# A whole encoder block on one core: later steps for the linear heads' functions, other pages for the embedding, another start of the value weights, and two moved hand-overs

## The chip, the core and the metric

The kernel runs as one program on one core of one Trainium2 chip. The metric is the device time of one execution in microseconds (us). In the views of the profile PE is the engine of matrix products, ACT and DVE are the two engines of elementwise work, POOL is a third one that is little used here, and SP issues most of the transfers between HBM and the on-chip memory (SBUF). Everything is fp32.

## The reference

One layer of an encoder over 512 frames of 2048 values:

```python
h = rms_norm(x, norm_mix_w)
q_a, k_a, v_a, q_g, k_g, v_g, r_g, gate_lr = split_cols(h @ w_in, IN_SPLITS)
y_a = chunked_band_attention(...)          # 16 heads of 64, a learned bias by distance
log_a = log_sigmoid(gate_lr @ w_gla_gate_up + b_gla_gate) / 16
o_g = gated_linear_attention(q_g, k_g, v_g, log_a)      # 4 heads, chunks of 64
y_g = rms_norm(o_g, gla_norm_w) * silu(r_g)
x = x + concatenate([y_a, y_g]) @ w_out
h = rms_norm(x, norm_ffn_w)
u = causal_depthwise_conv(h @ w_ffn_up, w_ffn_conv, b_ffn_conv)   # width 3, 11264 channels
u_gate, u_val = split(u, 2)
x = x + (gelu(u_gate) * u_val) @ w_ffn_down
g = sigmoid(rms_norm(x, norm_ple_w) @ w_ple_gate)
x = x + g * (p @ w_ple_proj)               # the embedding
return rms_norm(x, final_norm_w)
```

## The kernel before

**Products.** A product of large matrices is cut into units of 256 output columns (of the weight's 128-column blocks, two of them), and a unit is computed by seven block products instead of eight, with sums and differences of quarters of the weight and of the input. The seven are P1, P2, P6, P5, P7, P3, P4 in this order. Each needs one block of weights (L11, L12, S1 to S4, L22: quarters or their sums) and one operand made from the input (R11, R21, N1, N2, T3, R22, T4). An operand is kept in two halves of four tiles, g = 0 and g = 1. In the programs' names in_T, up_R or dn_N are such operands of the stages in, up and dn; accA, accB and accC are the three accumulators; u is a unit's output page.

**Splits.** To reach fp32 accuracy each block of weights (a page `l` or `s`) and each operand is split into a high part, which ACT copies, and a low part, which DVE makes by a subtraction. Both go into one page `wsplit` of a ring of three (w0 to w2), starting at a float of the page that SHIFT gives: 3 for ordinary units, 29 for value units (kind "v"), 48 for the embedding and for the first projection of the values (wtile). The pages themselves start at multiples of 64 bytes. Each block product is then 24 matmuls of 128x128 by 256 columns: high by high, high by low, low by high for eight tiles.

**Stages.** In order: the first projection (rows with L239 to L241) with the input norm; the low-rank gate; the stage `linear` (units 16, 20, 21, 17, 22, 23, 18, 8, 19, of which 20 to 23 are value units, in which the split weight is the streamed operand of the matmul); `front` (attention units 0 to 7 and units 9 to 11); the embedding (four units, PSUM tiles `pp`, output pages `pp_o`, stored to a scratch `ppd` in HBM); `wo`, the output projection; `up` with 44 units and a convolution (pages `cv`); `dn0`, `dn1`, `dn2`, the three parts of the down projection; `pg`, the gate of the embedding; the last norm. The stages wo, up and pg are chained: the last two column blocks of an operand's half g = 1 are not loaded from scratch but split straight from the tiles of the units just computed ("tails").

**What sets the order.** The main loop runs over steps, one block product each. Everything else is put into an agenda: a list of (k, function) for each step. In a step the functions with k = 0 come first, then the high part of the weight two steps ahead (ACT), then the functions with k from 1 to under 2, then its low part (DVE), then the product (PE), then the functions with larger k, then the collect, in which ACT copies or DVE adds the accumulator into the page u. ACT, DVE and PE keep the order in which the program is written. SP's transfers are ordered by the scheduler of the tile layer from the same program, and a transfer waits on SP for its data and its page.

**What is touched.** `gla_head` gives the functions of a linear head: `load_v`, `logits`, `softplus` (e: Abs, Exp, Ln), `least`, `sums` (a scan into cs), `powers` (eb, en, dd, dec: exponentials of cs), `decays`, each at a step of its unit (`gates_begin`); then the head's products from `normed` to `result`, with the root of its norm (`root`: Ln and Exp; `root_exact`), and at last the store of the head's output (ond). `after_up` gives a unit of up its scaling, the three taps of its convolution, Gelu, the gate and the store. `embedding` copies the sums of `pp` into `pp_o`. `attend` is the attention of a front unit, with its bias page. A table at the end of front places wo's operands (`kept` is the half whose page holds the embedding's input `ps` until then). Rings of pages are named by tags: u0 to u3, c0 to c2, r0 to r8, w0 to w2, x0, x1.

Of the kernel before, what the change touches and what calls it, by code (L numbers as in the profile page):

```python
# [34 lines left out]
SHIFT = {"v": 29, "pp": 48}  # L35
# [8 lines left out]
def encoder_block(ctx: ExitStack, tc: tile.TileContext, A, out):  # L44
# [604 lines left out]
    def after_up(unit):  # L649
        f = unit.u  # L650

        def scale():
            vec.tensor_tensor(unit.o, unit.o, rb2, ALU.mult)
            unit.c = page("c", "cv").rearrange("p (s t) -> p s t", s=2)

        def tap(s, j):
            blk = s * FB + f
            u, c = unit.o[:, s, :], unit.c[:, s, :]
            if j == 2:
                act.activation(c, u, AF.Identity, scale=cw[:, blk, 2:3], bias=cw[:, blk, 3:4])  # L660
            else:
                d = 2 - j
                vec.scalar_tensor_tensor(c[:, d:], u[:, :T - d], cw[:, blk, j:j + 1], c[:, d:], ALU.mult, ALU.add)

        def gate():
            g = unit.c[:, 1, :]
            vec.tensor_tensor(g, unit.c[:, 0, :], g, ALU.mult)

        def join():
            ci, k, second = unit.slot  # L670
            if second:
                store_pair(gd[ci], k, held[0], unit.c[:, 1, :])
            else:
                held[0] = unit.c[:, 1, :]

        return [(0, 1, scale), (0, 2, lambda: [tap(0, 2), tap(1, 2)]), (1, 1, lambda: [tap(0, 1), tap(0, 0)]),
                (1, 2, lambda: act.activation(unit.c[:, 0, :], unit.c[:, 0, :], AF.Gelu_apprx_tanh)),
                (2, 1, lambda: [tap(1, 1), tap(1, 0)]), (3, 1, gate), (4, 1, join)]
# [39 lines left out]
    def embedding(unit):  # L718

        hi, lo = unit.w["PP"]  # L720
        for i in range(4):
            if i % 2 == 0:
                o = page("c", "pp_o").rearrange("p (s t) -> p s t", s=2)
# [14 lines left out]
    def attend(unit):  # L738
# [6 lines left out]
        def load_e():  # L745
            for s in range(2):
                nc.sync.dma_start(bias[0][:, s, :], A["bias"][2 * b + s])
# [136 lines left out]
    def gla_head(unit):  # L884
# [11 lines left out]
        def softplus():  # L896
# [3 lines left out]
            act.activation(e, e, AF.Ln, bias=1.0)  # L900
# [13 lines left out]
        def powers():  # L914
            for n, k in (("eb", 1.0), ("en", -1.0)):
                M[n] = gt(n, n)
                act.activation(M[n], M["cs"], AF.Exp, scale=k / TAU)
            act.activation(M["dd"], M["dd"], AF.Exp, scale=-1.0 / TAU)
# [11 lines left out]
        def gates_begin():  # L930
            i = base[unit]
            for t, k, f in ((0, 0, load_v), (0, 6, logits), (1, 2, softplus), (1, 3, least), (2, 1, sums), (2, 2, powers),
                            (4, 1, decays)):
                agenda[i + t].append((k, f))
# [77 lines left out]
        def root():  # L1012
            M["rg"] = gt("rg", "cs")
            act.activation(M["rg"], M["ms"], AF.Ln, scale=1.0 / 256, bias=epst)
            act.activation(M["rg"], M["rg"], AF.Exp, scale=-0.5)
# [9 lines left out]
        def result():  # L1025
            for vb in range(2):
# [6 lines left out]
                (7, 3, root_exact), (8, 1, result), (10, 0, lambda: nc.sync.dma_start(ond[hd], M["o"]))]  # L1033
# [65 lines left out]
    for a, b in zip(stages[3:], stages[4:]):  # L1099
        i0 = base[a.units[-1]]  # L1100
        for n, p in enumerate(PLAIN):
            op = PRODUCTS[p][1]
            for g in range(2):
# [4 lines left out]
                if g and b.chained and op in ("R21", "T4"):  # L1108
                    at = max(at, 15)
# [13 lines left out]
    for n, p in enumerate(PLAIN):  # L1123
        op = PRODUCTS[p][1]
        for g in range(2):
            kept = (op, g) == ("N1", 1)
            agenda[i0 + (11 if kept else n + 1)].append((0, lambda op=op, g=g: wo.load(op, g)))
            agenda[i0 + (13 if kept else n + 4)].append((3, lambda op=op, g=g: wo.split(op, g, True, (0,) if g else ())))
        at, k = ((9, 1), (9, 1), (10, 1), (14, 1), (13, 3), (14, 3), (15, 3))[n]
# [13 lines left out]
    agenda[i0 + 5].append((1, lambda: embedding_split(raws["p"], xtile("N1", 1, "ps"))))  # L1143
# [181 lines left out]
    def open_attention():  # L1325
        gctx.close()
        att.append(actx.enter_context(tc.tile_pool(name="att", bufs=1, side="right", reuse_waits="tile")))
        bias.append(pg.tile([P, 2, T], F32, tag="r7", name="bias"))

    agenda[base[front.units[0]] + 8].append((1.5, open_attention))  # L1330
# [187 lines left out]
```

## Time and profile before

| | us |
|---|---|
| median of 3 runs | 2262.68 (2260.53 to 2263.29) |
| profiled execution | 2261.3 |
| its span, first to last instruction | 2259.6 |
| PE busy | 2202.8 (97%) |
| DVE busy | 1938.2 (86%) |
| ACT busy | 1345.1 (60%) |
| mean granted clock of PE | 0.992 |

In the rows of a timeline the first number is the start in us from the span's start, the second the duration, then the engine, the line, the operation, and the tiles it writes and reads; x24 is the number of equal instructions in a run; what stands in brackets is the idle time of the engine before it and what ended it. Most instructions have line 64, a helper that records them, so the tiles tell them apart. For matmuls the first tile behind the arrow is the streamed operand, the second the stationary one. A row's duration ends after the last matmul's drain, so the spacing of matmuls is taken from one start to the next.

### The profile page before, as it was taken

Reading aid. Unit: us, or ns where it says so; the run is one execution under the profiler, and the core shown is the slowest. Engines: PE = TensorE matmul, PEld = TensorE weight load, DVE = VectorE, ACT = ScalarE, POOL = GpSimd, SP = SyncE. Lnnn points to the kernel's source line nnn. Section 1 sums busy time; section 2 is a strip of 40 time slices with the busy share of each in tenths; the row PEclk is TensorE's granted clock in tenths of the full one; section 3 lists DMA queues with packets and bytes.
Section 4 is the critical chain, followed back from the end, with each engine's and each line's share of the span. In section 5 each row is a group of like instructions: output and inputs, shape, how many; then the busy total and the mean of one; then the engine's idle time right before and its main releaser. Section 6 shows DMA issues by size and latency. Waiting matters only on the chain.

```text
span 2259.6 us, 46287 instructions
## 1 busy us (share of the span) xinstructions
PE 2202.8 (97%) x18588; PEld 2151.8 (95%) x18588; DVE 1938.2 (86%) x2655; ACT 1345.1 (60%) x2001; POOL 158.3 (7%) x196
## 2 busy tenths in 40 slices
PE   9999999999999999999999999999999999999995
PEld 8899988999989999999999999999999999999995
DVE  8476778999869898999888898889898797999997
ACT  9455556777666565555555555555564554766655
POOL 0000000000000010000000100000000100000000
PEclk9999999999999999999999999999999999999998
DMA  7466755677888987888888888888866967879994
GB/s 245 128 186 177 212 154 155 188 189 194 286 266 268 309 243 202 225 226 224 222 215 223 215 224 216 215 225 214 266 208 232 310 243 252 302 254 329 277 300 158
DMA packets 190760, 518.31 MB, mean 229 GB/s; under 512 B 20272, under 2 KB 66608, under 8 KB 190544
## 3 DMA queue, kind: packets, MB, share of 16 engines
q1 hardware_dynamic: 160272, 415.72, 54.1%
q0 software_dynamic: 25920, 93.33, 23.1%
q10 hardware_dynamic: 4352, 6.29, 0.8%
q8 instruction: 146, 2.39, 0.4%
q14 instruction: 70, 0.57, 0.1%
HBM read 441.86 MB, written 71.30 MB: 227 GB/s over the span
## 4 chain that ended last, share of the span: by engine, by line
PE 79%; DVE 8%; DMA 7%; ACT 3%; issue 2%; SPq 0%; ACTq 0%; DVEq 0%; POOLq 0%
PE accA L64 40%; PE accC L64 21%; PE accB L64 10%; DVE wsplit L64 2%; PE v L239 1%; PE v L240 1%; PE v L241 1%; DVE u L64 1%; DMA dn_R<-g_R 1%; PE py L64 1%; DMA ppd<-pp_o 1%; PE ptr L64 1%; DMA l<-in_w_ple_gate 1%; PE psc L64 1%; DMA pg_T<-h_T 1%
## 5 line engine op out<-in xcount | busy, mean ns | idle before, releaser
L64 ACT ACTIVATE wsplit<-l 128x1024 fp32r<-128x1024 f32 (+1 forms) x476 | 495.3, 1041 | 301.7 <-PE accC L64 129.8
L64 DVE TENSOR_TENSOR wsplit<-l,wsplit 128x1024 fp32r<-128x1024 f32 (+1 forms) x476 | 571.0, 1201 | 110.3 <-ACT wsplit L64 109.4
L64 DVE TENSOR_TENSOR wsplit<-s,wsplit 128x1024 fp32r<-128x1024 f32 (+1 forms) x253 | 303.5, 1201 | 59.6 <-ACT wsplit L64 59.1
L64 ACT ACTIVATE wsplit<-s 128x1024 fp32r<-128x1024 f32 (+1 forms) x253 | 262.5, 1038 | 62.1 <-PE accB L64 33.4
L64 ACT ACTIVATE u<-accA 128x256 f32<-128x256 f32 x302 | 113.8, 377 | 265.6 <-PE accA L64 265.5
L64 PE MATMUL accA<-up_T,wsplit 128*128 128x256 f32 x2112 | 253.2, 276 | 0.0
L64 PEld LDWEIGHTS accA<-up_T,wsplit 128*128 128x128 f32 x2112 | 245.6, 188 | 0.1
L64 DVE SCALAR_TENSOR_TENSOR cv<-u,cw,cv 128x511 f32<-128x511 f32 (+1 forms) x176 | 131.5, 747 | 3.1
L64 PE MATMUL accB<-up_R,wsplit 128*128 128x256 f32 x1056 | 129.3, 279 | 2.6 <-ACT up_R L64 1.4
L64 PE MATMUL accA<-dn_T,wsplit 128*128 128x256 f32 x1056 | 126.8, 277 | 3.8 <-DVE wsplit L64 2.1
L405 POOL DMA_DIRECT2D s<-in_w_up x88 | 76.1, 865 | 765.6 <-DMA s<-in_w_up 460.4
L64 PEld LDWEIGHTS accB<-up_R,wsplit 128*128 128x128 f32 x1056 | 124.9, 190 | 3.4 <-ACT up_R L64 1.6
L64 PEld LDWEIGHTS accA<-dn_T,wsplit 128*128 128x128 f32 x1056 | 122.8, 188 | 4.8 <-DVE wsplit L64 2.7
L64 PE MATMUL accA<-up_R,wsplit 128*128 128x256 f32 x1056 | 126.9, 276 | 0.0
L64 PE MATMUL accC<-up_R,wsplit 128*128 128x256 f32 x1056 | 126.5, 276 | 0.0
L64 PE MATMUL accA<-up_N,wsplit 128*128 128x256 f32 x1056 | 126.5, 276 | 0.0
L64 PE MATMUL accC<-up_N,wsplit 128*128 128x256 f32 x1056 | 126.5, 276 | 0.0
L64 PEld LDWEIGHTS accA<-up_R,wsplit 128*128 128x128 f32 x1056 | 122.9, 188 | 0.5 <-ACT u L64 0.2
L64 PEld LDWEIGHTS accC<-up_N,wsplit 128*128 128x128 f32 x1056 | 122.8, 188 | 0.0
L64 PEld LDWEIGHTS accC<-up_R,wsplit 128*128 128x128 f32 x1056 | 122.8, 188 | 0.0
L64 PEld LDWEIGHTS accA<-up_N,wsplit 128*128 128x128 f32 x1056 | 122.8, 188 | 0.0
L64 PE MATMUL accA<-in_T,wsplit 128*128 128x256 f32 x768 | 97.8, 284 | 9.0 <-ACT u L64 7.5
(337 smaller groups left out, 4244.2 us busy)
## 6 DMA issues: line engine op xcount, KB each, us to landing
l<-in_w_up SPq DMA_DIRECT2D x132, 512.0 KB, 4.5
s<-in_w_up SPq DMA_DIRECT2D x88, 512.0 KB, 5.0
s<-in_w_up POOLq DMA_DIRECT2D x88, 512.0 KB, 6.0
l<-in_w_dn SPq DMA_DIRECT2D x56, 448.0 KB, 5.2
l<-in_w_blk SPq DMA_DIRECT2D x48, 512.0 KB, 4.6
s<-in_w_blk SPq DMA_DIRECT2D x32, 512.0 KB, 4.4
s<-in_w_blk POOLq DMA_DIRECT2D x32, 512.0 KB, 7.6
l<-in_w_out SPq DMA_DIRECT2D x28, 512.0 KB, 5.1
```

The costliest lines, as they stand in the source:

```text
L64: ins = f(*args, **kw)
L239: nc.tensor.matmul(ps[t], x[:, 0, sl], wh, start=kt == 0, stop=False)
L240: nc.tensor.matmul(ps[t], x[:, 0, sl], wl, start=False, stop=False)
L241: nc.tensor.matmul(ps[t], x[:, 1, sl], wh, start=False, stop=kt == KD - 1)
L405: nc.gpsimd.dma_start(t, src("L22" if name == "S1" else "L11"), accum_op=ALU.add)
```

## The change

1. Value units' split weights start at float 32 of their page instead of 29.
2. For the last three units of up, whose work goes into the start of dn0, the scaling, the taps, Gelu, the gate and the store come up to two steps later or are spread.
3. The embedding's second output page of unit 0 is taken from tag u0, and that of unit 1 from u3. The other six rotate through c0 to c2.
4. The bias page of the attention is taken at the first load of a bias, and the pool of the attention opens at step 9 instead of 8.
5. In a linear head, softplus' logarithm is a function of its own, half a step later; the sums go from (2, 1) to (3, 1); the powers from (2, 2) to (4, 1), with dd and dec apart at (4, 3); the decays from (4, 1) to (6, 1). The root's exponential is a function of its own at (8, 1); root_exact, the result and the store come a step later each.
6. The embedding's input lies in the second half of T3 instead of N1, so that N1's half is loaded early and T3's at step 14, with its split after step 16.
7. In up and pg the split of R21's second half comes after step 14 instead of 15.

The diff:

```diff
-SHIFT = {"v": 29, "pp": 48}
+SHIFT = {"v": 32, "pp": 48}
...
+        if unit.pos - len(unit.stage.units) in unit.stage.late:
+            return [(0, 1, scale), (1, 1, lambda: [tap(0, 2), tap(1, 2)]), (2, 1, lambda: [tap(0, 1), tap(0, 0)]),
+                    (3, 1, lambda: act.activation(unit.c[:, 0, :], unit.c[:, 0, :], AF.Gelu_apprx_tanh)),
+                    (3, 3, lambda: [tap(1, 1), tap(1, 0)]), (4, 1, gate), (5, 1, join)]
         return [(0, 1, scale), (0, 2, lambda: [tap(0, 2), tap(1, 2)]), (1, 1, lambda: [tap(0, 1), tap(0, 0)]),
                 (1, 2, lambda: act.activation(unit.c[:, 0, :], unit.c[:, 0, :], AF.Gelu_apprx_tanh)),
                 (2, 1, lambda: [tap(1, 1), tap(1, 0)]), (3, 1, gate), (4, 1, join)]
...
-                o = page("c", "pp_o").rearrange("p (s t) -> p s t", s=2)
+                spare = {(0, 2): (pg, "u0"), (1, 2): (late[0], "u3")}.get((unit.u, i))
+                o = (spare[0].tile([P, 1024], F32, tag=spare[1], name="pp_o") if spare else page("c", "pp_o")).rearrange("p (s t) -> p s t", s=2)
...
         def load_e():
+            if not bias:
+                bias.append(pg.tile([P, 2, T], F32, tag="r7", name="bias"))
...
-            act.activation(e, e, AF.Ln, bias=1.0)
+
+        def logs():
+            act.activation(M["e"], M["e"], AF.Ln, bias=1.0)
...
+
+        def falls():
             act.activation(M["dd"], M["dd"], AF.Exp, scale=-1.0 / TAU)
...
-            for t, k, f in ((0, 0, load_v), (0, 6, logits), (1, 2, softplus), (1, 3, least), (2, 1, sums), (2, 2, powers),
-                            (4, 1, decays)):
+            for t, k, f in ((0, 0, load_v), (0, 6, logits), (1, 2, softplus), (1, 3, least), (2, 2, logs), (3, 1, sums),
+                            (4, 1, powers), (4, 3, falls), (6, 1, decays)):
...
             act.activation(M["rg"], M["ms"], AF.Ln, scale=1.0 / 256, bias=epst)
+
+        def rooted():
             act.activation(M["rg"], M["rg"], AF.Exp, scale=-0.5)
...
-                (7, 3, root_exact), (8, 1, result), (10, 0, lambda: nc.sync.dma_start(ond[hd], M["o"]))]
+                (8, 1, rooted), (8, 3, root_exact), (9, 1, result), (11, 0, lambda: nc.sync.dma_start(ond[hd], M["o"]))]
...
-                    at = max(at, 15)
+                    at = max(at, 14 if op == "R21" else 15)
...
-            kept = (op, g) == ("N1", 1)
-            agenda[i0 + (11 if kept else n + 1)].append((0, lambda op=op, g=g: wo.load(op, g)))
-            agenda[i0 + (13 if kept else n + 4)].append((3, lambda op=op, g=g: wo.split(op, g, True, (0,) if g else ())))
-        at, k = ((9, 1), (9, 1), (10, 1), (14, 1), (13, 3), (14, 3), (15, 3))[n]
+            kept = (op, g) == ("T3", 1)
+            agenda[i0 + (14 if kept else n + 1)].append((0, lambda op=op, g=g: wo.load(op, g)))
+            agenda[i0 + (16 if kept else n + 4)].append((3, lambda op=op, g=g: wo.split(op, g, True, (0,) if g else ())))
+        at, k = ((9, 1), (9, 1), (10, 1), (12, 1), (16, 3), (14, 3), (15, 3))[n]
...
-    agenda[i0 + 5].append((1, lambda: embedding_split(raws["p"], xtile("N1", 1, "ps"))))
+    agenda[i0 + 5].append((1, lambda: embedding_split(raws["p"], xtile("T3", 1, "ps"))))
...
-        bias.append(pg.tile([P, 2, T], F32, tag="r7", name="bias"))
-
-    agenda[base[front.units[0]] + 8].append((1.5, open_attention))
+
+    agenda[base[front.units[0]] + 9].append((1.5, open_attention))
```

Where it moves instructions, at three places.

ACT in unit 19, the last of the stage linear, from the split for P6 on. Before (rg is the root of the head before, e the softplus of this one, eb to dec its powers; u<-u is the gate's Silu, u<-accA the collects of P1 and P6):

```order
L64 ACT_TABLE_LOAD
L64 ACTIVATE rg<-rg 128x512
L64 ACT_TABLE_LOAD
L64 ACTIVATE u<-u 128x1024
L64 ACTIVATE u<-accA 128x256
L64 ACTIVATE wsplit<-s_2885 128x1024
...
L64 ACTIVATE wsplit<-s_2926 128x1024
L64 ACT_TABLE_LOAD
L64 ACTIVATE eb<-cs 128x512
L64 ACTIVATE en<-cs 128x512
L64 ACTIVATE dd<-dd 128x512
L64 ACTIVATE dec<-cs 128x8
L64 ACTIVATE u<-accA 128x256
```

And in the changed kernel:

```order
L64 ACT_TABLE_LOAD
L64 ACTIVATE u<-u 128x1024
L64 ACTIVATE u<-accA 128x256
L64 ACTIVATE wsplit<-s_2885 128x1024
L64 ACT_TABLE_LOAD
L64 ACTIVATE rg<-rg 128x512
...
L64 ACTIVATE e<-e 128x512
L64 ACTIVATE u<-accA 128x256
L64 ACTIVATE wsplit<-l_2719 128x1024
L64 ACTIVATE u<-accC 128x256
...
L64 ACTIVATE eb<-cs 128x512
```

The root's exponential has moved behind the collect of P1, and the powers from ahead of P6's collect to behind P5's.

DVE at the start of up, where the tails of the operands' second halves are split. Before:

```order
L64 TENSOR_TENSOR up_N_9121<-up_N_9121 128x1024
L64 TENSOR_TENSOR l_8982<-l_8982,s_9092 128x1024
L64 SCALAR_TENSOR_TENSOR tp<-tp,u 128x256
L64 TENSOR_TENSOR wsplit<-l_9059,wsplit 128x1024
L64 TENSOR_TENSOR up_R_9021<-up_R_9021 128x512
L64 TENSOR_TENSOR up_R_9021<-u,up_R_9021 128x256 x2
L64 TENSOR_TENSOR up_N_9087<-up_N_9087 128x512
```

In the changed kernel:

```order
L64 TENSOR_TENSOR up_R_9021<-up_R_9021 128x512
L64 TENSOR_TENSOR up_R_9021<-u,up_R_9021 128x256 x2
L64 TENSOR_TENSOR up_N_9121<-up_N_9121 128x1024
L64 TENSOR_TENSOR l_8982<-l_8982,s_9092 128x1024
L64 SCALAR_TENSOR_TENSOR tp<-tp,u 128x256
L64 TENSOR_TENSOR wsplit<-l_9059,wsplit 128x1024
L64 TENSOR_TENSOR up_N_9087<-up_N_9087 128x512
```

R21's split (up_R) has moved ahead of a whole operand half, a sum of weights and a weight's low part; the rows are the same ones.

ACT at the hand-over from up to dn0, around the splits for P7 of the first pair. Before:

```order
L64 ACTIVATE cv<-u,cw 128x512 x2
L64 ACTIVATE dn_T_19450<-dn_T_19450 128x1024
L64 ACTIVATE u<-accA 128x256
L64 ACTIVATE wsplit<-s_19387 128x1024
L64 ACTIVATE cv<-cv 128x512
L64 ACTIVATE dn_T_19548<-dn_T_19548 128x1024
```

In the changed kernel:

```order
L64 ACTIVATE dn_T_19450<-dn_T_19450 128x1024
L64 ACTIVATE u<-accA 128x256
L64 ACTIVATE wsplit<-s_19387 128x1024
L64 ACTIVATE cv<-u,cw 128x512 x2
L64 ACTIVATE dn_T_19548<-dn_T_19548 128x1024
```

The convolution's first taps (cv<-u,cw) stand behind the split of T3 and of the weight instead of ahead of them, and Gelu (cv<-cv) has gone further back.

## The prediction

> **What bounds it now.** I read the page's engine shares first, then the chain that ended last, then PE's timeline for every place where the spacing of matmuls is above the usual.
>
> ```profile
> PE 2202.8 (97%) x18588; PEld 2151.8 (95%) x18588; DVE 1938.2 (86%) x2655; ACT 1345.1 (60%) x2001; POOL 158.3 (7%) x196
> PE 79%; DVE 8%; DMA 7%; ACT 3%; issue 2%; SPq 0%; ACTq 0%; DVEq 0%; POOLq 0%
> ```
>
> PE is the bound of the whole: PE's order and its count of matmuls do not change, so only two things can move the end: matmuls that run closer together, and waits of PE that go away or come new. The change is five such edits, and I price each where it acts.
>
> **Value units (start of the halves 29 to 32 floats).** In a value unit the split weight is the streamed operand, written first in a row's pair; in the others it is the stationary one.
>
> ```profile
> 92.75 0.39 PE L239 MATMUL v<-wv_s,in_R 128*128 128x512 f32 x1
> ...
> 95.24 0.39 PE L241 MATMUL v<-wv_s,in_R 128*128 128x512 f32 x1
> ...
> 109.44 2.88 PE L64 MATMUL accA<-in_N,wsplit 128*128 128x256 f32 x24
> 112.16 2.88 PE L64 MATMUL accC<-in_N,wsplit 128*128 128x256 f32 x24
> ...
> 156.04 5.92 PE L64 MATMUL accA<-wsplit,in_T 128*128 128x256 f32 x48
> 161.80 5.92 PE L64 MATMUL accC<-wsplit,in_R 128*128 128x256 f32 x48
> ```
>
> Ordinary: 112.16 − 109.44 = 2.72 us for 24, 113.3 ns each. Value: 161.80 − 156.04 = 5.76 for 48, 120.0 ns. The excess of 6.7 ns is 1/17 of 113.3, the time of about 15 of 256 columns, or some 60 bytes of a row: as if one 64-byte piece more were read because the row starts inside a piece. The pages start at multiples of 64 bytes; 29 floats are 116 bytes, which is no multiple, 32 are 128, which is. The first projection supports this: there too a split weight is streamed, out of the same pages, but from float 48 (192 bytes), and eleven steps take 95.24 − 92.75 = 2.49 us, 226 ns per 512 columns, 113 per 256. So it is not the streaming of a split weight as such. There are 4 units x 7 products x 24 = 672 such matmuls: 672 x 6.7 ns = **4.5 us**. Bounds: 0 (another cause) and 4.5. I take 4.5.
>
> The Trainium skill, "TensorE: Matmul & The Clock Gate", "Back-to-back issue gap", gives N / 2.4 + 2.5 ns for a warm matmul, 109.2 for 256 columns, with no term for the start address; the rows' 113.3 and 120.0 are both above it. By that rule this edit is worth 0, which is rival A.
>
> **Gates and heads of the linear units.** In each of these units PE's P7 waits for ACT, which is in a run of table loads, logarithms and exponentials ahead of the collect of P6.
>
> ```profile
> 115.83 2.99 PE L64 MATMUL accA<-in_T,wsplit 128*128 128x256 f32 x24 [0.78 <-ACT u L64]
> 182.90 2.88 PE L64 MATMUL accC<-in_N,wsplit 128*128 128x256 f32 x24
> 185.93 3.03 PE L64 MATMUL accA<-in_T,wsplit 128*128 128x256 f32 x24
> ...
> 310.13 5.45 PE L64 MATMUL accA<-in_T,wsplit 128*128 128x256 f32 x24 [5.06 <-ACT u L64]
> 315.41 2.90 PE L64 MATMUL accC<-in_R,wsplit 128*128 128x256 f32 x24
> ```
>
> Unit 16 loses 115.83 − 112.16 − 2.72 = 0.95, unit 17 185.93 − 182.90 − 2.72 = 0.31, and I give unit 18 the same: 1.6 us. The same ACT items spread over later steps can hide behind the products P5 to P4, whose steps have none of them now; their readers, the products with keys and queries, come a unit later. I take 1.6 (bounds 0.5 and 1.6). The last unit, 19, is the large one: the wait of 5.06, and then 24 matmuls in 315.41 − 310.13 = 5.28 instead of 2.72, at half clock. It also carries the root of the head before. ACT's rows there, and one stretch with each engine's busy time (PE, PEld, DVE, ACT):
>
> ```profile
> 297.96 1.06 ACT L64 ACTIVATE u<-u 128x1024 f32<-128x1024 f32 x1
> 298.93 0.36 ACT L64 ACTIVATE u<-accA 128x256 f32<-128x256 f32 x1
> 308.03 0.63 ACT L64 ACTIVATE eb<-cs 128x512 f32<-128x512 f32 x1 [1.08 <-DVE cs L64]
> 309.71 0.36 ACT L64 ACTIVATE u<-accA 128x256 f32<-128x256 f32 x1
> ...
> 297.00:310.00 13.00, 7.63 (x65) 7.23 (x64) 12.65 (x18) 11.83 (x17) 0.86 (x1) 0.95 0.53 158
> ```
>
> Between the two collects (298.93 and 309.71) ACT now has 10.8 us. After the change the powers with their wait for the sums (308.03 to 309.71 and 1.08 ahead, 2.8 us) and a table load come behind P5's collect, and the root's exponential comes between the two collects instead of before the first, with a table load fewer there since Exp follows Exp: P1's collect moves to about 297.0, P6's to about 304.6, and P7 starts near 304.8 and at full clock. But the stretch shows DVE busy for 12.65 of 13.00 us: the same work must still pass DVE. From the gate's multiply to P7's low half it has 11.3 us of rows, so that half is done near 308.4, and P7's last 8 matmuls wait 1.9 us, P3's about 1 more. Front's first matmul falls at about 316.4 instead of 320.87: **4.4 us** (bounds 2.5, if the two new waits cost half clock too, and 5.0).
>
> **Front's second unit.** Head 19's tail falls under it, and a DVE queue that waits for a transfer:
>
> ```profile
> 361.91 3.00 PE L64 MATMUL accA<-in_T,wsplit 128*128 128x256 f32 x24 [1.63 <-ACT u L64]
> 370.44 3.12 PE L64 MATMUL accA<-in_T,wsplit 128*128 128x256 f32 x24 [1.19 <-DVE u L64]
> ...
> 368.65 0.17 DVE L64 MEMSET bias<- 64x128 f32 x1 [1.56 <-PE accC L64]
> ...
> 356.77 0.33 SPq L1033 DMA_DIRECT2D ond<-og  x1
> 360.93 0.86 SPq L747 DMA_DIRECT2D bias<-in_bias x2
> ```
>
> The 1.63 goes. But the head's result and its store (ond) move a step later: counted from front's start as before, I place the store at about 359.4, and the bias load stands behind it on SP, with a weight load and va's. On DVE the mask (368.65) waits for that load, and behind the mask P4's low half, P7's collect and P3's low half are queued; PE's P4 waits for them. With the landing at about 369 P4 starts near 371.1 where it was 370.44: **−0.7** (bounds −2.0, and +2.9 if the load lands as now).
>
> **Embedding and wo.** ACT copies the embedding's sums into pages of a ring whose stores have not landed yet, and PE waits for ACT:
>
> ```profile
> 618.20 5.74 PE L64 MATMUL pp<-ps,wsplit 128*128 128x512 f32 x24 [1.47 <-ACT pp_o L64]
> 625.86 7.32 PE L64 MATMUL pp<-ps,wsplit 128*128 128x512 f32 x24 [1.92 <-ACT pp_o L64]
> 634.81 3.02 PE L64 MATMUL pp<-ps,wsplit 128*128 128x512 f32 x12 [1.63 <-ACT pp_o L64]
> 638.36 3.02 PE L64 MATMUL pp<-ps,wsplit 128*128 128x512 f32 x12 [0.54 <-ACT pp_o L64]
> 641.22 5.62 PE L64 MATMUL accA<-wo_R,wsplit 128*128 128x256 f32 x48
> ...
> 628.02 1.09 ACT L64 ACTIVATE pp_o<-pp 128x512 f32<-128x512 f32 x2 [1.72 <-DMA ppd<-pp_o]
> 637.71 1.08 ACT L64 ACTIVATE pp_o<-pp 128x512 f32<-128x512 f32 x2 [2.47 <-DMA ppd<-pp_o]
> ```
>
> From 618.20 to 641.22 are 23.0 us for 72 matmuls of 512 columns, which need 72 x 0.2265 = 16.3: 6.7 lost, 1.9 of it half clock (7.32 for 24 instead of 5.4), the wait ahead of 618.20 (1.47) is ACT's for an operand of wo and stays. With two of the eight output pages taken from rings that are idle there (u0, u3), the copies at 628.02 and 637.71 no longer meet a page whose store is on its way, and the other uses of the c ring lie further apart. I keep 1.8 of the 6.7 as waits for what stays (page c0's return, wo's own splits on ACT): **4.9 us** (bounds 2.5 and 6.5). What is late next is wo's second product, which waits for ACT's splits either way. u3 is also wo's: its next owner writes it some 12 us after the store is issued, which covers a usual landing. T3's last half, the operand that now waits for the embedding's input to be done with, is loaded at step 14 and split after 16, which leaves two steps, 5.4 us, before its P7.
>
> **R21's split.** The two places where a chained stage starts:
>
> ```profile
> 803.25 1.48 PE L64 MATMUL accB<-up_R,wsplit 128*128 128x256 f32 x8 [1.38 <-ACT up_R L64]
> 805.98 6.33 PE L64 MATMUL accB<-up_R,wsplit 128*128 128x256 f32 x36 [1.26 <-DVE up_R L64]
> 833.91 0.95 PE L64 MATMUL ms<-ones,acc 128*128 128x1 f32 x8
> ...
> 2077.52 1.45 PE L64 MATMUL accB<-pg_R,wsplit 128*128 128x256 f32 x8 [2.26 <-ACT pg_R L64]
> ...
> 801.50:837.00 35.50, 32.86 (x268) 32.15 (x267) 34.28 (x49) 26.11 (x45) 1.72 (x2) 0.95 0.84 244
> 2074.20:2110.60 36.40, 32.86 (x270) 32.22 (x269) 35.43 (x51) 27.08 (x45) 2.59 (x3) 0.95 0.98 297
> ```
>
> PE's visible loss in up is 1.38 + 1.26, and half clock after it (36 matmuls in 6.33 where 36 x 0.113 is 4.1): some 5 us, and in pg, with 2.26 for 1.38, some 6. A split one step earlier removes most of these waits. But in the stretches from there to the norm's row sums DVE is busy for 34.28 of 35.50 and for 35.43 of 36.40 us, and PE's ms at 833.91 needs the last sum of squares that this DVE work ends in. The edit puts R21's halves ahead of N1's on DVE and takes nothing away: PE runs ahead and then waits at ms. What can be gained is part of DVE's idle 1.2 and 1.0, **0.3 us** for both (bounds −0.5 and 2.2; rival B has the full 11).
>
> **Up's last hand-overs.** At dn0's start ACT takes a convolution tap that waits for DVE, and dn_T's split stands behind it:
>
> ```profile
> 1664.54 2.12 PE L64 MATMUL accA<-dn_T,wsplit 128*128 128x256 f32 x16 [1.20 <-ACT wsplit L64]
> ...
> 1672.56 5.77 PE L64 MATMUL accC<-dn_R,wsplit 128*128 128x256 f32 x48
> ...
> 1698.06 1.19 PE L64 MATMUL accA<-dn_T,wsplit 128*128 128x256 f32 x8 [1.07 <-DVE wsplit L64]
> ...
> 1660.79 1.53 ACT L64 ACTIVATE cv<-u,cw 128x512 f32<-128x512 f32 x2 [2.31 <-DVE u L64]
> ```
>
> From 1664.54 to 1672.56 are 8.0 us for 48 matmuls that need 5.44: 2.6 lost, and 1.2 ahead of them, 3.8 in all. With the taps behind P7's splits on both engines I let 3.6 of it go (the convolution's reader, the store of the gated rows, is wanted by dn1 only). What moves on is DVE's: the pair's other taps now fall under the next unit's P7, which I let wait 1.4 instead of 1.07. **3.3 us** (bounds 2 and 4).
>
> **Sum.** 4.5 + 1.6 + 4.4 − 0.7 + 4.9 + 0.3 + 3.3 = 18.3 us. The profiled execution took 2261.3 (span 2259.6), 1.4 below the median of the runs, 2262.68: 2243.0 on its own scale, **2244** beside the median. With all lower bounds but the value term's, 4.5 + 0.5 + 2.5 − 2.0 + 2.5 − 0.5 + 2 = 9.5; with all upper ones 26.
>
> **Rivals.** A: the value rows do not change, their excess being that of the operands' roles or of another address rule. For it: no row shows a start at an odd multiple of 64 beyond these pages. Against: the first projection. 18.3 − 4.5 = 13.8: 2249.
>
> B: the R21 edit is worth PE's visible waits, because some of DVE's work before ms can be left for later. 18.3 + 11 = 29.3: 2233. The window rows speak against it.
>
> C: covers fail together. Each remaining wait above some 1.7 us costs half clock (1.92 did at 625.86; 1.47 and 1.63 did not), and stores, of which the embedding then has as many in less time, land later. Near the lower bounds, 9.5 to 11: 2252.
>
> D, slower: the bias load. DVE works in order, and its mask waits for the landing; every us beyond about 369 is one of PE's, since P4's low half and P7's collect stand behind. It eats the whole gain if the load lands 18 us later than I place it, behind the later store; 20 later would make 2264, 24 later 2268. The load was issued at 360.93 and its mask ran at 368.65, so such a landing is far from anything at this place.
>
> **How the numbers follow.** 2244 with its own range of 2238 to 2250: 0.55. A: 0.17. B: 0.06. C: 0.18, with a third of it above 2254. D: 0.04. The range for 8 in 10 is 2235 to 2254: it takes A and most of C in, and leaves B and D out. About 0.2%, 4.5 us, is what a measurement can tell: faster means below 2258. Faster: 0.55 + 0.17 + 0.06 + 0.15 = 0.93; same 0.04 (rest of C, start of D); slower 0.03.
>
> **What would show it.** Value rows of 48 start 5.44 us apart, not 5.76 (else A). The row with 5.06 on ACT is gone, and waits on DVE near 1.9 and 1 stand in its place. The pages' waits of 1.72 and 2.47 on ppd are gone. At the starts of up and pg the waits of accB fall while a new wait of about 5 us stands at ms or pb (without it, B). In dn0 the taps stand behind dn_T's splits. I am wrong in substance if PE shows a new wait above 3 us in a place not named here, or if the gain is under 9 us.

## The result and the profile after

The changed kernel takes 2254.02 us (median of 7 runs, 2252.18 to 2258.41), the one before 2262.68 beside it (median of 7, 2260.53 to 2267.88): a ratio of 0.9962 (95% interval 0.995 to 0.9973), 8.7 us faster where 18.3 were forecast. Two of the kernels below had one execution far longer than their others (5696.02 and 3319.83 us), which their ratios leave out. The page and PE's waits of the changed kernel (who waited for whom: us in total, times, longest):

```profile
PE 2196.4 (97%) x18588; PEld 2146.3 (95%) x18588; DVE 1937.3 (86%) x2655; ACT 1344.6 (60%) x2000; POOL 158.6 (7%) x196
...
PE accA L64 <- DVE wsplit L64: 7.7, 8, 2.9
PE ms L64 <- ACT q L64: 5.5, 2, 3.4
PE accA L64 <- DVE u L64: 5.0, 2, 4.7
PE pp L64 <- ACT pp_o L64: 4.7, 4, 1.7
PE accC L64 <- DVE wsplit L64: 4.5, 5, 2.0
```

PE's order has not changed, so each matmul of one trace has its partner in the other, and the difference of their starts, read along the program, says where time was won and lost:

| first matmul of | before | after | difference | won since the row above |
|---|---|---|---|---|
| unit 16 | 102.75 | 103.87 | +1.12 | −1.1 |
| unit 18 | 243.47 | 240.74 | −2.73 | 3.9 |
| unit 19 | 291.63 | 288.77 | −2.86 | 0.1 |
| front's first unit | 320.87 | 314.95 | −5.92 | 3.1 |
| the end of front | 608.60 | 606.40 | −2.20 | −3.7 |
| wo | 641.22 | 636.58 | −4.63 | 2.4 |
| up | 796.04 | 790.38 | −5.65 | 1.0 |
| up's third unit | 841.10 | 835.29 | −5.81 | 0.2 |
| dn0's third unit | 1704.53 | 1696.45 | −8.08 | 2.3 |
| pg's third unit | 2115.37 | 2107.30 | −8.06 | 0.0 |
| the last row sums | 2243.35 | 2236.49 | −6.86 | −1.2 |

The first and the last row are no part of the edits: in the other runs below unit 16 starts 0.1 to 1.8 us later than before, and the tail behind 2115 gives back up to 1.2. Each trace is one execution. Among the kernels below that run the same program in a stretch, unit 19 wins 3.1 in six of seven traces (1.8 in the seventh), front loses 2.6 to 4.5, embedding and wo together win 2.9 to 4.5, and up's end with dn0's start wins 1.1 to 3.1.

Three places differ most from the forecast. The value steps (PE's timeline, after):

```profile
132.90 3.01 PE L64 MATMUL accB<-wsplit,in_R 128*128 128x256 f32 x24
135.75 0.60 PE L64 MATMUL pkt<-ident,kd 128*128 128x128 f32 x4
...
155.33 5.82 PE L64 MATMUL accA<-wsplit,in_T 128*128 128x256 f32 x48
160.99 5.82 PE L64 MATMUL accC<-wsplit,in_R 128*128 128x256 f32 x48
```

48 matmuls now take 160.99 − 155.33 = 5.66 us, 117.9 ns each: better than 120.0, but not 113.3. Some steps have the whole gain (132.90: 24 up to 135.75, of which the spacing inside is 113.4); over the 28 steps, 8 run at 113.4 and 20 at 117.7.

Unit 19 and front's second unit (PE, DVE and SP's issues, after):

```profile
301.85 2.09 PE L64 MATMUL accA<-in_T,wsplit 128*128 128x256 f32 x16 [0.37 <-ACT u L64]
306.84 1.24 PE L64 MATMUL accA<-in_T,wsplit 128*128 128x256 f32 x8 [2.90 <-DVE wsplit L64]
307.90 4.50 PE L64 MATMUL accC<-in_R,wsplit 128*128 128x256 f32 x24
312.23 2.88 PE L64 MATMUL accA<-in_T,wsplit 128*128 128x256 f32 x24
...
353.57 3.00 PE L64 MATMUL accA<-in_T,wsplit 128*128 128x256 f32 x24
360.43 1.19 PE L64 MATMUL accC<-in_R,wsplit 128*128 128x256 f32 x8 [2.04 <-DVE wsplit L64]
367.24 5.46 PE L64 MATMUL accA<-in_T,wsplit 128*128 128x256 f32 x24 [4.70 <-DVE u L64]
```

```profile
298.00 0.75 DVE L64 TENSOR_SCALAR lf<-pz,cols 128x512 f32<-128x512 f32 x1 [1.30 <-ACT e L64]
304.25 1.40 DVE L64 SCALAR_TENSOR_TENSOR og<-og,cols,rg 128x512 f32<-128x512 f32 x2
305.57 1.22 DVE L64 TENSOR_TENSOR wsplit<-s,wsplit 128x1024 fp32r<-128x1024 f32 x1
...
365.48 0.17 DVE L64 MEMSET bias<- 64x128 f32 x1 [5.11 <-DMA bias<-in_bias]
```

```profile
353.79 0.33 SPq L1046 DMA_DIRECT2D ond<-og  x1
355.34 0.71 SPq L761 DMA_DIRECT2D va<-vad  x1
358.21 1.03 SPq L754 DMA_DIRECT2D bias<-in_bias  x2
...
SPq L754 <- DMA ond<-og: 2.1, 1, 2.1
```

The 5.06 of unit 19 is gone, and DVE's waits stand in its place, 2.90 where 1.9 was forecast, then P3 at half clock for most of its matmuls (24 in 4.33 us) where a second wait of about 1 was. In front's second unit the wait of P7 has gone, and one of 4.70 with half clock behind it (24 in 5.25) has come at P4.

### The profile page after: what moved, and what is told of

Read it like the earlier page. It is cut to its first block, busy times and chain, and to the rows that moved or that the text cites. A ratio compares the mean times of both kernels' runs of the same rounds, so it can differ in the third digit from the quotient of the medians.

```text
span 2252.8 us, 46290 instructions
## 1 busy us (share of the span) xinstructions
PE 2196.4 (97%) x18588; PEld 2146.3 (95%) x18588; DVE 1937.3 (86%) x2655; ACT 1344.6 (60%) x2000; POOL 158.6 (7%) x196
## 4 chain that ended last, share of the span: by engine, by line
PE 80%; DVE 9%; DMA 4%; ACT 4%; issue 2%; ACTq 0%; SPq 0%; DVEq 0%
PE accA L64 41%; PE accC L64 21%; PE accB L64 10%; DVE wsplit L64 3%; PE v L240 1%; PE v L239 1%; PE v L241 1%; ACT wsplit L64 1%; DVE u L64 1%; DMA dn_R<-g_R 1%; PE py L64 1%; PE ptr L64 1%; PE psc L64 1%; DMA ppd<-pp_o 1%; DVE l L64 1%
## 5 line engine op out<-in xcount | busy, mean ns | idle before, releaser
L64 DVE TENSOR_TENSOR wsplit<-l,wsplit 128x1024 fp32r<-128x1024 f32 (+1 forms) x476 | 570.5, 1200 | 114.7 <-ACT wsplit L64 113.3
```

The costliest lines, as they stand in the source:

```text
L64: ins = f(*args, **kw)
```

## The experiments

Twelve kernels, each timed beside the kernel before. Its medians there lie from 2261.55 to 2263.60, so the ratio (in brackets, with its interval) is what compares two of the kernels; ratios that differ by less than about 0.0017 are not told apart.

**The value start alone.** Edit, on the kernel before:

```diff
-SHIFT = {"v": 29, "pp": 48}
+SHIFT = {"v": 32, "pp": 48}
```

> The kernel before with the value start alone moved from float 29 to 32. In the changed kernel 8 of the 28 value steps run at 113.4 ns a matmul and 20 at 117.7, where before all had 120. If the start alone does that, this run has the same two paces in the same steps and is 192 x 6.6 + 480 x 2.3 ns = 2.4 us faster than before (2260.3), with every wait elsewhere as before. If the pace came from the other edits (what ACT and DVE do meanwhile), the value steps stay at 120 ns and the time at 2262.7.

Measured: 2259.14 (ratio 0.9989, 0.998 to 0.9997), 2.4 below its 2261.55. The row at 156.02 runs 48 in 5.66 us, as in the changed kernel:

```profile
156.02 5.82 PE L64 MATMUL accA<-wsplit,in_T 128*128 128x256 f32 x48
161.68 5.82 PE L64 MATMUL accC<-wsplit,in_R 128*128 128x256 f32 x48
```

The start alone does it, with 7 of the 28 steps at 113.4 here instead of 8, and it is worth half of the forecast.

**Another multiple of 64 bytes.** Edit, on the changed kernel:

```diff
-SHIFT = {"v": 32, "pp": 48}
+SHIFT = {"v": 48, "pp": 48}
```

> The changed kernel with the value start at float 48 instead of 32. The pages begin at an odd multiple of 64 bytes, so 32 floats put the streamed rows on an odd multiple of 64 and 48 floats on a multiple of 128, as in the first projection. Theory 128: all 28 value steps take 113.3 ns a matmul, 480 x 4.4 ns = 2.1 us less than the changed kernel (2251.9). Theory phase: the pace depends on how weight load and stream fall against each other and not on this start; then 20 steps keep 117.7 ns and the time stays at 2254.

Measured: 2254.93 (0.9966, 0.9953 to 0.9978), and all 28 value steps at 120.0 ns (119.5 to 120.0):

```profile
155.57 5.92 PE L64 MATMUL accA<-wsplit,in_T 128*128 128x256 f32 x48
161.33 5.92 PE L64 MATMUL accC<-wsplit,in_R 128*128 128x256 f32 x48
```

Neither theory: a start at a multiple of 128 bytes is as slow as float 29. This also takes away the forecast's witness, since the first projection starts its tiles at this very float 48.

**A scan of starts.** Edit, on the changed kernel:

```diff
+SCAN = {20: {"P1": 0, "P2": 8, "P6": 16, "P5": 24, "P7": 40, "P3": 16, "P4": 3},
+        22: {"P1": 16, "P2": 40, "P6": 24, "P5": 8, "P7": 24, "P3": 8, "P4": 0}}
+FIRST = (48, 32, 16, 0, 40, 24, 8, 3)
...
             at = SHIFT.get(unit.kind, 3)
+            if unit.kind == "v":
+                at = SCAN[unit.u // 2 * 2][prod]
+            elif unit.kind == "pp":
+                at = (48, 32, 3, 16)[unit.u % 4]
```

> The changed kernel with other starts of the split weights, and nothing else: in the value units 0, 8, 16, 24, 40, 3 (units 20 and 21) and 16, 40, 24, 8, 24, 8, 0 (22 and 23) floats, one start for each product; in the first projection 48, 32, 16, 0, 40, 24, 8, 3 in turn over its tiles; in the embedding 48, 32, 3, 16 for its four units. Theory: what changes is a fixed time for each matmul beside its columns (113.3 for 256 and 226.5 for 512 columns are 0.42 ns a column with 5 to 7 and 13 ns on top), large or small by where the streamed row and the stationary one start against each other; then 512-column matmuls have two paces too, some 220 and 226.5 ns, and starts of one class (equal up to 128 bytes) share a pace in all three places. Rival: the fixed time belongs to the columns (0.443 ns each), the first projection and the embedding keep 226.5 ns at every start, and only value steps differ. No effect on the total is expected beyond 3 us either way.

Measured (one run): 2255.97. In the value units the means per matmul are 113.3 (start 0, P1) and 117.7 (start 0, P4), 119.8 (8), 118.6 (16), 118.6 (24), 118.4 (40), 117.7 (3). Each start stands in one or two products there, so only 29, 32 and 48, which were tried in all 28 steps, compare cleanly for 256 columns. In the first projection's second pass, where nothing waits, 512 columns take 226.9 (48), 233.4 (32), 230.9 (16), 228.9 (0), 233.1 (40), 234.2 (24), 232.9 (8), 228.8 ns (3). In the changed kernel all these tiles start at float 48 and take 226.6. So the start sets the pace there too, float 48 is the best of the eight for 512 columns and, in the run above, as slow as 29 for 256, and starts that agree modulo 128 bytes (16 and 48) do not agree in pace. In the embedding the split weight is the stationary operand, and there too the pace follows its start: 226.6 (48), 229.0 (32), 233.5 (3) and 233.3 (16), where the changed kernel has 226.7 in all four units. So it is not the streamed row alone. Both theories fall in this form, and the 226.5 for 512 columns told nothing of 256. What rule joins the two operands' starts, the length and the two paces of one start is open.

**The mask of the bias.** Edit, on the changed kernel:

```diff
-items = [..., (3, 1, low), (4, 1, mask), (5, 0, load_v), ...]
+items = [..., (3, 1, low), (5, 3, mask), (5, 0, load_v), ...]
```

> The changed kernel with DVE's mask of the bias a step and a half later, behind two low halves and a collect instead of ahead of them; nothing else moves. Theory: this in-order wait (5.1 us of DVE for the bias load, then 4.7 of PE at 367.24 and 24 matmuls at half clock) is the largest missing piece of the forecast; without it PE's wait and the half clock go, and since the load lands at 365.2 and its first reader came at 369.6, nothing takes their place: 5 to 7 us faster than the changed kernel, 2248. Rival: the wait only moves to the first reader of the bias on DVE or to the scores' banks, and the time stays within 1.5 us of 2254.

Measured: 2248.87 (0.9939, 0.9926 to 0.9951), 5 below the changed kernel (its highest run, 2250.69, is below that kernel's lowest, 2252.18), and the lowest median of all. PE's P4 and DVE's mask now:

```profile
362.15 2.91 PE L64 MATMUL accA<-in_T,wsplit 128*128 128x256 f32 x24
...
364.86 0.17 DVE L64 MEMSET bias<- 64x128 f32 x1 [2.14 <-DMA bias<-in_bias]
```

P4 follows the scores at once and at full clock; the mask still waits for the load, with nothing behind it that P4 needs. The loss was that of the in-order queue on DVE, not of the load.

**The whole edit of the linear heads undone.** Edit, on the changed kernel:

```diff
-... (2, 2, logs), (3, 1, sums), (4, 1, powers), (4, 3, falls), (6, 1, decays)
+... (1, 2, logs), (2, 1, sums), (2, 2, powers), (2, 2, falls), (4, 1, decays)
-... (8, 1, rooted), (8, 3, root_exact), (9, 1, result), (11, 0, <store>)
+... (7, 1, rooted), (7, 3, root_exact), (8, 1, result), (10, 0, <store>)
```

> The changed kernel with the linear heads' functions at their old steps (softplus, sums, powers, decays, root, result and store), all other edits kept. By the forecast's terms the edit is worth 1.6 + 4.4 - 0.7 = 5.3 us: 2259.3. Theory from the trace: 1.6 in units 16 to 18, 3.1 in unit 19, and 4 lost again in front's second unit, where the bias load waits for the later store of the head's output: 0 to 1.5 us in all, 2254 to 2255.5, with PE's 5 us wait back in unit 19 and the 4.7 us wait in front gone.

Measured: 2253.20 (0.9955, 0.9941 to 0.9968): no worse than with the edit. At unit 16 and at the end of front this trace stands at +0.14 and −3.33 against the kernel before, the changed kernel at +1.12 and −2.20: 3.5 us won from there to there without the edit, 3.3 with it. The wait in unit 19 is back and that in front small:

```profile
307.90 5.40 PE L64 MATMUL accA<-in_T,wsplit 128*128 128x256 f32 x24 [5.06 <-ACT u L64]
...
367.51 2.98 PE L64 MATMUL accA<-in_T,wsplit 128*128 128x256 f32 x24 [0.47 <-DVE u L64]
```

The largest edit of the change, forecast at 5.3 us, is worth nothing as it stands: it wins 4.6 up to front's first unit (7.0 against 2.4) and gives it back in the second one.

**DVE's work of unit 19 in other places.** Three edits on the mask's run. First, the result behind the low half of its step:

```diff
-(9, 1, result)
+(9, 3, result)
```

> The mask's run with one more edit: each head's result (1.4 us of DVE) behind the low half prepared in its step instead of ahead of it, so that in unit 19 P7's low half is 1.4 us earlier. Theory: PE's wait there falls from 2.9 to 1.5 us, short enough that P3 runs at full clock (1.6): 2 to 3 us below the mask's run, 2246 to 2247. Rival: P3's low half, behind the result and the sums on DVE, stays where it is, so P3 waits instead: within 1 us of 2248.9.

Measured: 2253.14 (0.9956, 0.9942 to 0.9969), 4.3 above the mask's run where even the rival had 1. The mechanism is the rival's:

```profile
304.53 1.19 PE L64 MATMUL accA<-in_T,wsplit 128*128 128x256 f32 x8 [1.59 <-DVE wsplit L64]
309.57 1.86 PE L64 MATMUL accC<-in_R,wsplit 128*128 128x256 f32 x8 [2.04 <-DVE wsplit L64]
...
373.46 1.25 PE L64 MATMUL ptr<-ident,sc 128*128 128x128 f32 x8 [3.10 <-DVE sc L64]
```

P7's wait falls to 1.59, P3's low half waits 2.04 instead, and the last head's result, later too, holds its store, the bias load and so the first softmax: PE waits 3.10 for it, 1.31 in the mask's run.

Second, root and result of all heads but the last behind the low halves for P7 and P3, and the sums and powers a step later:

```diff
-(3, 1, sums), (4, 1, powers), (4, 3, falls) ... (8, 3, root_exact), (9, 1, result), (11, 0, <store>)
+(4, 3, sums), (5, 1, powers), (5, 3, falls) ... (9, 3, root_exact), (10, 3, result), (12, 0, <store>)
```

> The changed kernel with DVE's mask later as in the run before of that edit, and in the linear heads the exact root and the result behind the low halves for P7 and P3 (all heads but the last), and the sums, powers and falls a step later. Theory: in unit 19 PE waited 2.9 us for P7's low half and then ran P3 at half clock (1.6), because 4.2 us of root and result stand ahead of it on DVE, and 2.6 of sums ahead of P3's; behind the low halves they hide under P3, P4 and the next unit: 3.5 to 4.5 us beside the mask's 5 to 6, so 2244 to 2246. Rival: DVE's work only moves, P4 or the next unit's first products wait instead, or the heads' products (which now get their powers a step later) wait, and the time is that of the mask alone, 2248 to 2250.

Measured: 2251.80 (0.9949, 0.9937 to 0.9962), not told apart from the mask's run and not faster. P7's and P3's waits are gone, and the sums stand ahead of P7's collect, for whose bank P4 waits:

```profile
305.85 3.15 PE L64 MATMUL accC<-in_R,wsplit 128*128 128x256 f32 x24
313.29 5.46 PE L64 MATMUL accA<-in_T,wsplit 128*128 128x256 f32 x24 [4.29 <-DVE u L64]
```

Third, all of it behind that collect:

```diff
-(3, 1, sums), (4, 1, powers), (4, 3, falls) ... (8, 3, root_exact), (9, 1, result), (11, 0, <store>)
+(5, 4, sums), (5, 5, powers), (5, 5, falls) ... (12, 1, root_exact), (12, 3, result), (13, 0, <store>)
```

> As the run with sums and mask, but DVE's exact root, result, sums and the powers behind the collect of P7 and the low half for P4 (the run before had put the sums ahead of that collect, so that P4 waited 4.5 us for its bank). Theory: in unit 19 PE then waits under 1 us from P7 to P4 and runs at full clock, front's first unit starts some 4 us earlier than in the mask's run, and 4.2 + 2.6 us of DVE work hide under front's first two products, at the price of up to 1.5 us at their low halves: 2.5 to 4 us below the mask's run (2248.9), 2245 to 2246.5. Rival: DVE, busy for nearly all of this stretch, is the bound, and front's first products or the heads' products (their powers come later still) wait for what P7 to P4 no longer wait for: 2248 or more.

Measured: 2262.27 (0.9996, 0.9987 to 1.0004). Now each of units 16 to 18 pays, where the head's first products need the powers:

```profile
132.83 0.46 PE L64 MATMUL pat<-eb,en 128*128 128x128 f32 x2 [2.57 <-DVE eb L64]
```

That costs 9.8 us from unit 16 to 19, where the mask's run wins 4.0. Unit 19 itself goes as the theory has it, with one wait of 0.37 at P7, but in front the second product waits 2.33 for ACT and the powers' readers 0.84 for DVE. From unit 19's start to the end of front the mask's run wins 3.4 us against before and the three edits win −1.2, 1.1 and 3.7: none wins more than 0.3 beyond the mask, and each place has a reader that waits. This fits DVE as the bound of the stretch. The third edit for unit 19 alone, which would spare units 16 to 18, was not run.

**R21's split back at step 15.** Edit, on the changed kernel:

```diff
-at = max(at, 14 if op == "R21" else 15)
+at = max(at, 15)
```

> The changed kernel with R21's second half split after step 15 again in up and pg. Theory: DVE's work up to the norm's row sums is the bound there, so this costs 0.1 to 0.6 us (2254.5), with PE's waits back at accB (1.4, 1.3 and 2.3, 1.3) and the small waits on low halves behind them gone. Rival: PE's waits at accB are on the path, then it is 5 + 6 = 11 us slower, 2265.

Measured: 2252.87 (0.9956, 0.9944 to 0.9968): not told apart from the changed kernel. From up's first to its third unit this run loses 0.30 against before, where the changed kernel wins 0.16. The same matmuls in the changed kernel and in this run, up's start:

```profile
795.60 4.70 PE L64 MATMUL accB<-up_R,wsplit 128*128 128x256 f32 x40
804.40 3.03 PE L64 MATMUL accA<-up_N,wsplit 128*128 128x256 f32 x24 [0.55 <-DVE wsplit L64]
812.01 3.90 PE L64 MATMUL accC<-up_N,wsplit 128*128 128x256 f32 x32 [0.87 <-DVE wsplit L64]
834.73 1.13 PE L64 MATMUL pb<-dg,ones 128*128 128x512 f32 x2 [0.41 <-DVE dg L64]
```

```profile
796.68 1.46 PE L64 MATMUL accB<-up_R,wsplit 128*128 128x256 f32 x8 [1.38 <-ACT up_R L64]
799.41 7.00 PE L64 MATMUL accB<-up_R,wsplit 128*128 128x256 f32 x36 [1.28 <-DVE up_R L64]
834.37 1.02 PE L64 MATMUL pb<-dg,ones 128*128 128x512 f32 x2
```

Some 5 us of waits and half clock at accB are gone with the edit and come back as small waits for DVE's low halves; pb is reached 44.4 us after up's first matmul with the edit and 44.9 without it. Rival B is out. The forecast's wait of about 5 us at ms or pb has not come either (0.41 at pb): DVE holds PE all along the way, not at its end.

**The embedding's pages back to the ring.** Edit, on the changed kernel:

```diff
-spare = {(0, 2): (pg, "u0"), (1, 2): (late[0], "u3")}.get((unit.u, i))
+spare = {}.get((unit.u, i))
```

> The changed kernel with all eight output pages of the embedding from the ring c0 to c2 as before. If the pages were the cause of ACT's stops, as forecast, the embedding loses its 3.3 us again: 2257.5. Theory of the issue: the stops at the third and the fifth store are there either way; what returns is the wait of single copies for a page, 0.5 to 1.5 us: 2255.

Measured: 2255.21 (0.9968, 0.9957 to 0.998), 1.2 above the changed kernel, which the times do not tell apart. From the end of front to up's first unit this trace wins 1.65 us against before, the changed kernel 3.45: the pages are worth 1.8 there in these two executions. All of this run's 1.65 is won behind wo's first product; whether it comes with the kept operand in T3 was not tried.

**The stores issued by POOL.** Edit, on the changed kernel:

```diff
-nc.scalar.dma_start(ppd[...
+nc.gpsimd.dma_start(ppd[...
```

ACT in the changed kernel, where it stops twice:

```profile
621.67 1.06 ACT L64 ACTIVATE pp_o<-pp 128x512 f32<-128x512 f32 x2
625.92 0.37 ACTq L736 DMA_DIRECT2D ppd<-pp_o  x1
626.33 1.09 ACT L64 ACTIVATE pp_o<-pp 128x512 f32<-128x512 f32 x2 [3.59 <-DMA ppd<-pp_o]
```

> The changed kernel with the embedding's eight stores issued by POOL instead of ACT. Theory: ACT, which is in order, stops not for a page but at the issue of the third and the fifth store, until the first and the second have landed (issue at 625.92, first landing at 625.84; issue at 632.19, second landing at 632.12); on POOL these stops hold up no copy, and PE's waits for pp_o of 1.67 and 1.02 go: 2 to 3.5 us faster than the changed kernel, 2251. Rival: the copies then wait for the pages of the same stores, or POOL's weight loads behind them come late, and the time is within 1 us or above.

Measured: 2256.01 (0.9974, 0.9963 to 0.9984), 2 above the changed kernel and not below it. PE, then ACT, in this run:

```profile
614.30 16.79 PE L64 MATMUL pp<-ps,wsplit 128*128 128x512 f32 x72 [0.97 <-ACT pp_o L64]
642.29 8.41 PE L64 MATMUL accB<-wo_R,wsplit 128*128 128x256 f32 x48 [5.75 <-ACT wsplit L64]
...
633.58 1.09 ACT L64 ACTIVATE pp_o<-pp 128x512 f32<-128x512 f32 x2 [4.27 <-DMA ppd<-pp_o]
638.44 1.09 ACT L64 ACTIVATE pp_o<-pp 128x512 f32<-128x512 f32 x2 [3.77 <-DMA ppd<-pp_o]
```

Both were right for a while. The embedding runs 72 matmuls without a gap, so ACT did stop at the store's issue (621.67 + 1.06 is 622.7, and the issue is at 625.92) and not for its page. The trace shows why: the program lets the third store tell of its landing by the semaphore (a counter that engines wait on) of the first, number 105, so ACT waits for the first's landing, 625.84, before it issues the third; the fifth and the second share 109 (landing 632.12, issue 632.19). But then the last unit's copies, earlier now than their pages are free, stop ACT for 4.27 and 3.77 us ahead of wo's splits, and wo's second product waits 5.75. From the end of front the embedding is 6.9 us ahead of before at wo's first product and 0.4 at up's, so the landings of the stores bind under both.

**Up's last units as before.** Edit, on the changed kernel:

```diff
-        if unit.pos - len(unit.stage.units) in unit.stage.late:
+        if False:
```

> The changed kernel with up's last three units handed over as before (taps ahead of P7's splits), all other edits kept. Theory, as forecast: this edit is worth about 3 us at dn0's start (the trace has 2.9 between 1662 and 1694): 2257, with PE's waits of 1.2 and 0.5 on ACT's split at the start of dn_T back. Rival: DVE is the bound of the hand-over as it is at the start of up, and the time stays within 1 us of 2254.

Measured: 2256.03 (0.997, 0.9958 to 0.9982), 2.0 above the changed kernel, which the times alone do not tell apart; the traces show the place. Between up's third unit and dn0's third the changed kernel wins 2.3 against before and this run nothing (−6.45 at the one, −6.46 at the other), with the wait back:

```profile
1658.07 2.12 PE L64 MATMUL accA<-dn_T,wsplit 128*128 128x256 f32 x16 [1.20 <-ACT wsplit L64]
```

## Why the prediction was right or wrong

The sign was right, the sum twice too large, and the time fell just above the range. By its own last sign, a gain under 9 us, the forecast was wrong in substance. Two terms failed most: the value start, 2.4 instead of 4.5, and front's second unit, −3.7 instead of −0.7. By its steps:

| step | forecast | traces and runs |
|---|---|---|
| value start | 4.5 | 2.4 (the start alone) |
| gates of units 16 to 18 | 1.6 | 1.6 (3.98 from unit 16 to 19, less 2.37 in the run with the heads undone) |
| unit 19 | 4.4 | 3.1 |
| front's second unit | −0.7 | −3.7 over front |
| embedding and wo | 4.9 | 3.4 |
| R21's split | 0.3 | 0.2 in the trace, 0.5 against the run without it |
| up's hand-overs | 3.3 | 2.3 |

The right column adds to 9.3; the first and the last row of the table of differences, which belong to no edit, take 2.3 of it in this execution. Rival C, the covers that fail together, came nearest with 2252, in part by luck: it keeps the value start at 4.5, and most other terms stayed above the lower bounds that it takes. Two sums are slightly off: the upper bounds add to 26.7, not 26, and unit 19's own rows, from P7 at 304.8, add to 315.9 for front's first matmul, not 316.4.

**Wrong: the value start's witness.** The step from the first projection (113 ns per 256 columns, so not the streaming of a split weight) treated 226.5 ns for 512 columns as the same pace as 113.3 for 256. With float 48 the value steps take 120.0. So what fell is the step from a row that starts inside a piece of 64 bytes to the whole excess of 6.7 ns: a start at a multiple of 64 bytes takes off 6.6 in 8 of 28 steps, 2.3 in 20, and nothing at float 48. Rival A's second half, another address rule, was nearer the truth, and the rule is open. With other starts the rows, a stream with a weight load for each matmul, have 113.3 to 120.0 for 256 columns and 226.9 to 234.2 for 512, so the count of columns alone does not give the pace here. The Trainium skill, "TensorE: Matmul & The Clock Gate", "Back-to-back issue gap", gives the isolated gap of a matmul by its count of columns alone.

**Wrong: front's second unit, rival D's mechanism.** The forecast named the queue (mask, low half, collect) and gave it 0.7. It read the bias load as standing behind the store on SP. In the kernel both use the page r7: the load waits not for the store's issue but for its landing (SP's wait of 2.1, landing at 358.15, load issued at 358.21), and it landed at 365.24, 50.3 us after front's first matmul where the forecast's 369, against 320.87, is 48.1. And it left out the half clock behind such a wait (24 matmuls in 5.25), though it had just read the same in unit 19. The lower bound of −2.0 was too tight for an event whose condition, a later store, the edit itself made. With it, the heads' edit is worth nothing, and moving the mask by a step and a half is worth 5 us.

**Off in size: unit 19.** The wait on DVE was 2.9 instead of 1.9, since DVE itself stood 1.3 us for ACT (298.00) in a stretch whose rows the forecast summed rightly (11.2 us without that wait, 11.3 forecast) but as if it never waited. The half clock behind the 2.9 is not what was lost. The run with up's last units as before has the same program up to here and the same wait, and full clock behind it (mean granted clock 1.00 from 307 to 312, 0.66 in the changed kernel):

```profile
306.93 1.22 PE L64 MATMUL accA<-in_T,wsplit 128*128 128x256 f32 x8 [2.91 <-DVE wsplit L64]
310.65 1.18 PE L64 MATMUL accC<-in_R,wsplit 128*128 128x256 f32 x8 [0.69 <-DVE wsplit L64]
312.21 2.97 PE L64 MATMUL accA<-in_T,wsplit 128*128 128x256 f32 x24 [0.38 <-DVE u L64]
315.02 2.88 PE L64 MATMUL accA<-in_R,wsplit 128*128 128x256 f32 x24
```

There PE waits for DVE in P3 and P4 instead, about the 1 us that the forecast had, and front starts 8.09 us after these last eight matmuls of P7, 8.11 in the changed kernel. DVE sets the end of unit 19 either way.

**Off in size and partly in cause: the embedding.** The rows at 628.02 and 637.71 name a store, and the forecast read them as waits for a page. The first of them is the wait at a store's issue (third store ready at 626.29, issued at 627.60, the first landed at 627.53), which other pages do not cure; the second is a page's. The sign that both waits on ppd go did not come: the changed kernel has 3.59 and 1.16 of them. The run with POOL shows that the landings bind in the end.

**Right:** the gates; R21's split with DVE as the bound (B had the visible 11 us), though not where PE would wait; the direction and place of dn0's gain, with the next unit's P7 waiting 1.37 where 1.4 was forecast; and the view that only PE's pace and its waits set the end.

## What to carry to other kernels

Before a step is moved later, follow its page as well as its queue: who else has that page, and whether the next owner needs the landing of a store rather than its issue. Where an in-order engine is busy for nearly a whole stretch, work moved on it goes from one reader's wait to the next one's; what paid here was to move the instruction that itself waits (a mask) behind those that others wait for. A pace read from matmuls of one shape is no witness for another shape.

## What the hardware showed that was not expected

The starts of its operands in their pages change the pace of a matmul of the split pages (type fp32r in the rows) by up to 6%, in an order that differs for 256 and 512 columns (48 floats: 120.0 of 113.3 to 120.0, and 226.9 of 226.9 to 234.2), and not for the streamed operand alone (226.6 to 233.5 by the stationary one's start, in the embedding). One start can have two paces (113.4 and 117.7) that repeat in the same steps of most runs. The start does not decide between them: in the run with up's last units as before, whose program up to there is the changed kernel's, the first of the eight quick steps ran at the slow pace.

The length of a wait alone did not decide whether half clock followed. Up to the last 25 us of a trace, the granted clock falls to 0.5 for about 3.41 us or twice or three times that (307.90 to 311.32 and 365.93 to 372.76 in the changed kernel, 361.30 to 371.54 with R21's split back at step 15). This followed waits of 1.92 us in the kernel before and 2.04 us in the run with the result moved (at 309.57), but not one of 2.63 us in the kernel before (at 2227.99), nor that of 2.91 us above. So the 1.7 us of rival C is no threshold. The Trainium skill, "TensorE: Matmul & The Clock Gate", "What's actually happening", has the array cold after at least one idle window of about 3.4 us; the length of the stretches at half clock agrees with that window, but the waits of 1.92 and 2.04 are shorter than it and half clock followed them.
